# Row maxima of two attention heads at a time, from matmuls on the two halves of TensorE's rows

## The chip, the cores and the metric

The kernel runs on one core of a Trainium2 chip. The metric is the device time of one execution in microseconds (us). Times are shown as the median of several runs; one further execution was taken with the profiler on, and all rows below come from it.

## The reference

One layer of a hybrid decoder, 2048 tokens of width 1024 behind 16 learned meta tokens (L = 2064 rows), in float32:

```python
h = layer_norm(concat(meta, x))
q, k, v, f_logit, g_att, u, g_pool = split(h @ w_in)
# forgetting attention, 16 heads of 64
c = cumsum(log_sigmoid(f_logit + b_f))              # per head, along the rows
s = q @ k.T / 8 + c[:, None] - c[None, :]           # causal
a = softmax(s) @ v * silu(g_att)
# pooling mixer: trailing means over 2, 4, 8, 16 rows, a small linear map, a scale
p = multiscale_pool(u) * silu(g_pool)
out = layer_norm(alpha * h + concat(a, p) @ w_out)[16:]
```

What the change touches is the softmax. For its exponentials the kernel wants, for each row of q, the largest logit beforehand. The term c of the query's own row is the same for all keys of the row and drops out; the term of the key, −c, does not, and has to be in the maximum.

## The kernel before

Matrix products are made to float32 precision out of pairs: each operand is split into a high part (hh, wh, ka, qa; float32r, which TensorE reads) and a low part (hl, wl, lo), and `mm3` issues three matmuls for one product (high by high, low by high, high by low).

The program has three stages. First the input is normalised and transposed, and v is projected (to about 290 us). Then comes the stretch of the projections (about 328 to 1290 us), which the change touches. Then the attention itself, which reads q, k and the maxima back from a DRAM tensor kqd, with the output projection filled in between (from about 1320 us).

In the second stretch a list of jobs is worked off in order. Each job projects 128 columns of w_in over all rows, in chunks (`proj`): 8 steps k, each one `mm3`, into one of two PSUM tiles d. Jobs are: `qk_job`, 16 times, one a head (64 columns of k beside 64 of q, five chunks of 412 or 416 rows); `gp_job` and `u_job`, 8 times each (gate and input of the pooling mixer); `ga_job`, 8 times (gate of the attention). gp_job and ga_job have four chunks of 512 rows, u_job five of 412 or 416. Weights of the next job are fetched and split in the middle of the job before.

After each chunk `qk_job` evicts k and q: ScalarE writes the high parts into ka and qa, VectorE the low parts into lo, and three transfers bring them to kqd. ka and qa have 64 rows of the head and two more: rows 64 and 65 of ka hold the key's forget term in two parts (loaded from kqd), those of qa are ones. So one matmul of 66 rows gives the logits with the forget term in them.

The maxima are found in pieces (`max_piece`): a row block i of 128 queries against the keys of a range p of up to 1024 positions. Range 0 starts at position 112, so block i has 128i + 144 keys over its ranges. A piece is one or two matmuls (512 columns at most each) into a PSUM tile mx of 1024 columns, of which there are two; VectorE adds a causal mask to the last 128 columns of a block's last range (mask_q), and one TENSOR_REDUCE over the piece writes a column of mxs. `max_end` joins the ranges, transposes the 16 columns and sends them to kqd rows 258 and 259.

Pieces are spread between the projection's steps: a queue `pend`, and `tick()` behind every step, which collects a credit and takes an entry off the queue for each whole credit. The credit of a step is 0.3, or, outside of a head's own job ("tail"), the length of the queue over the steps that are left until the next head's first chunk, if that is more. What is left then is emptied at once. [...]

## Time and profile before

| what | value |
|---|---|
| time, median of 3 runs | 2349.0 us (2347.35 to 2353.8) |
| the profiled execution: time, span | 2348.34 us, 2346.6 us |
| TensorE matmul busy | 2266.2 us, 97% of the span |
| VectorE, ScalarE, GpSimd busy | 1464.9, 978.3, 783.6 us |
| granted TensorE clock, mean | 0.99 |
| matmuls into mx (maxima) | 704 |
| reductions mxs<-mx on VectorE | 416, 359.5 us |

Busy time of an engine is the time in which at least one of its instructions is under way. Matmuls overlap in the array, so the listed length of one (its way through the pipeline) is longer than the time by which it holds up the next; that time is the distance between two starts. PEld are the loads of the stationary operand, which each matmul has. The helper that records every instruction gives them all one line, L86, so groups are told apart by their tiles.

### The profile page before, as it was taken

Reading aid. Unit: us, or ns where it says so; the run is one execution under the profiler, and the core shown is the slowest. Engines: PE = TensorE matmul, PEld = TensorE weight load, DVE = VectorE, ACT = ScalarE, POOL = GpSimd, SP = SyncE. Lnnn points to the kernel's source line nnn. Section 1 sums busy time; section 2 is a strip of 40 time slices with the busy share of each in tenths; the row PEclk is TensorE's granted clock in tenths of the full one; section 3 lists DMA queues with packets and bytes.
Section 4 is the critical chain, followed back from the end, with each engine's and each line's share of the span. In section 5 each row is a group of like instructions: output and inputs, shape, how many; then the busy total and the mean of one; then the engine's idle time right before and its main releaser. Section 6 shows DMA issues by size and latency. Waiting matters only on the chain.

```text
span 2346.6 us, 32233 instructions
## 1 busy us (share of the span) xinstructions
PE 2266.2 (97%) x11146; PEld 1902.4 (81%) x11146; DVE 1464.9 (62%) x2360; ACT 978.3 (42%) x1895; POOL 783.6 (33%) x624
## 2 busy tenths in 40 slices
PE   6999999999999999999999799999999999999998
PEld 4878799999999999999888577777777777776787
DVE  5521246755766567656634388787878777767347
ACT  4421421222212212211111387878878877776000
POOL 4700021222313404140010146555565655545000
PEclk9999999999999999999999899999999999999999
DMA  6743532222222222222222766675767767555955
GB/s 228 226 140 105 154 97 63 91 65 85 89 63 91 82 72 85 62 96 81 80 69 70 194 188 195 192 212 171 201 193 200 207 194 222 167 163 178 290 186 168
DMA packets 347778, 335.41 MB, mean 143 GB/s; under 512 B 57888, under 2 KB 271344, under 8 KB 347584
## 3 DMA queue, kind: packets, MB, share of 16 engines
q1 hardware_dynamic: 347616, 333.37, 47.0%
q8 instruction: 88, 1.44, 0.3%
q14 instruction: 74, 0.61, 0.1%
HBM read 209.15 MB, written 124.13 MB: 142 GB/s over the span
## 4 chain that ended last, share of the span: by engine, by line
PE 90%; DVE 3%; DMA 2%; issue 2%; ACT 2%; POOL 1%; SPq 0%; DVEq 0%; ACTq 0%; POOLq 0%
PE d L86 61%; PE s L86 11%; PE yo L86 7%; PE mx L86 6%; PE xo L86 5%; DVE pl L86 1%; PE fz L86 1%; PE tr L86 1%; DMA xm<-xa 1%; ACT ph L86 1%; DMA wst<-in_wout_dram 0%; SPq L86 0%; POOL acc L86 0%; ACT s L86 0%; POOL araw L86 0%
## 5 line engine op out<-in xcount | busy, mean ns | idle before, releaser
L86 PE MATMUL d<-hh,wh 128*128 128x412 f32 (+2 forms) x1472 | 543.6, 369 | 0.0
L86 PE MATMUL d<-hl,wh 128*128 128x412 f32 (+2 forms) x1472 | 538.3, 366 | 0.0
L86 PE MATMUL d<-hh,wl 128*128 128x412 f32 (+2 forms) x1472 | 537.9, 365 | 0.0
L86 DVE TENSOR_TENSOR pl<-s,ph 128x512 fp32r<-128x512 f32 (+3 forms) x592 | 373.5, 649 | 166.8 <-ACT s L86 158.2
L86 DVE TENSOR_REDUCE mxs<-mx 128x1 f32<-128x912 f32 (+14 forms) x416 | 359.5, 865 | 85.9 <-PE mx L86 76.1
L86 ACT ACTIVATE ph<-s 128x512 fp32r<-128x512 f32 (+3 forms) x592 | 336.9, 569 | 156.4 <-PE s L86 141.9
L86 PE MATMUL d<-wh,xm 128*128 128x512 f32 x1024 | 348.1, 397 | 4.2 <-DMA xm<-xa 3.4
L86 ACT ACTIVATE s<-s 128x512 f32<-128x512 f32 (+3 forms) x592 | 335.7, 567 | 0.0
L86 PEld LDWEIGHTS d<-hl,wh 128*128 128x128 f32 x1472 | 277.7, 189 | 24.8
L86 PEld LDWEIGHTS d<-hh,wh 128*128 128x128 f32 x1472 | 276.9, 188 | 23.0 <-ACT gst L86 0.3
L86 PEld LDWEIGHTS d<-hh,wl 128*128 128x128 f32 x1472 | 276.6, 188 | 23.3
L86 POOL TENSOR_TENSOR wl<-wst,wh 128x1024 fp32r<-128x1024 f32 x40 | 96.2, 2405 | 589.7 <-ACT wh L86 564.1
L86 PE MATMUL s<-qa,ka 68*128 68x512 f32 (+3 forms) x640 | 244.8, 383 | 21.5 <-DVE pl L86 21.1
L86 PE MATMUL yo<-pl,vt 128*66 128x512 f32 (+3 forms) x640 | 229.1, 374 | 11.3 <-ACT c L86 11.0
L86 PE MATMUL s<-qb,kb 128*128 128x512 f32 (+3 forms) x640 | 234.6, 367 | 0.0
L86 PE MATMUL xo<-ph,vt 128*128 128x512 f32 (+3 forms) x640 | 232.6, 367 | 0.0
L86 PEld LDWEIGHTS d<-wh,xm 128*128 128x128 f32 x1024 | 193.7, 190 | 47.1 <-issue 4.2
L86 POOL TENSOR_TENSOR tu<-ph 128x512 f32<-128x512 f32 x144 | 188.3, 1308 | 99.5 <-ACT ph L86 95.4
L86 PE MATMUL d<-wl,xm 128*128 128x512 f32 x512 | 203.1, 397 | 0.0
L86 PE MATMUL mx<-ka,qa 66*128 66x512 f32 (+5 forms) x704 | 198.2, 348 | 3.4 <-ACT qa L86 3.4
L86 PEld LDWEIGHTS s<-qa,ka 68*128 68x128 f32 x640 | 122.4, 191 | 61.4 <-DVE pl L86 33.7
L86 DVE TENSOR_TENSOR mx<-mx,mask_q 128x128 f32<-128x128 f32 x256 | 76.5, 299 | 117.8 <-PE mx L86 115.1
(185 smaller groups left out, 3097.4 us busy)
## 6 DMA issues: line engine op xcount, KB each, us to landing
xm<-xp SPq DMA_DIRECT2D x32, 1024.0 KB
xm<-xa SPq DMA_DIRECT2D x20, 1024.0 KB
vd<-vs SPq DMA_DIRECT2D x32, 512.0 KB
vt<-vd SPq DMA_DIRECT2D x64, 256.0 KB
qb<-kqd SPq DMA_DIRECT2D x64, 256.0 KB
xa<-am SPq DMA_DIRECT2D x32, 512.0 KB
xp<-pm SPq DMA_DIRECT2D x32, 412.0 KB
kqd<-lo SPq DMA_DIRECT2D x64, 206.0 KB
```

Source lines behind the costliest of these rows:

```text
L86: return in_order(f(*a, **k))
```

## The change

`k_job` and `q_job` take the place of `qk_job`, 8 times each, one pair of heads g: the first projects 128 columns of k (two heads), the second 128 of q. Head 2g lies on rows 0 to 63 of the tiles kp and qr, head 2g+1 on rows 64 to 127. A chunk is evicted by one ScalarE and one VectorE instruction, and four transfers bring it to kqd.

A piece now serves both heads. Their matmuls, of 64 rows each, are issued in turn, the first head's into one mx tile and the second's into the other; there are still two such tiles. The rows of the forget term are gone. Instead the term is kept in DRAM as fk, a row for each head, and `fb_load` brings the range that is due, broadcast to 128 partitions, into fb0 and fb1 (one buffer each). For each head VectorE adds the mask as before and then runs one tensor_tensor_reduce: logits plus fb, written back to the mx tile, with the maximum read out into mxs.

The pieces of range 0 are queued while q is projected, at 0.2 credits a step; then come the load of range 1, two empty entries, the nine pieces of range 1, the load of range 2, an empty entry, its one piece, and the end: of these 26 pieces a pair six fall into the q job. The queue is empty during k_job. The jobs between the pairs are three (gp, u, ga) for groups 0 to 5, two (gp, u) for group 6 and four for group 7, of which the last is done when the pools of the attention are open. The first job is now k_job 0 in place of gp_job 0; the forget chain runs inside it. The buffer pm of the pool job is one where it was two.

```diff
     kqd = dtile("kqd", [H, 260, L], F32)
+    fk = dtile("fk", [H, L], F32)
...
+        dma(fk.rearrange("h (s t) -> (h s) t", s=8), zf)
...
-        sched["credit"] += max(0.3, len(pend) / max(sched["steps"], 1) if sched["tail"] else 0.0)
+        sched["credit"] += max(sched["rate"], len(pend) / max(sched["steps"], 1) if sched["tail"] else 0.0)
...
+                fbs[e] = fbp.tile([P, 1024], F32, tag=f"fb{e}", name="fb")
+                dma(
+                    fbs[e][:, lo - 1024 * p : hi - 1024 * p],
+                    fk[2 * g + e : 2 * g + e + 1, lo - 112 : hi - 112].broadcast_to([P, hi - lo]),
+                )
...
-            ps = psm.tile([P, 1024], F32, tag="mx", name="mx", bufs=2)
+            pss = [psm.tile([P, 1024], F32, tag="mx", name="mx", bufs=2) for e in range(2)]
             v = lo
             while v < hi:
-                e = min(hi, 512 * (v // 512 + 1))
-                diag = e == P * i + 256
-                mm(
-                    ps[:, v - base : e - base], qa[:, NM + P * i : NM + P * (i + 1)],
-                    ka[:, v - 112 : e - 112], start=True, stop=True,
-                )
-                if diag:
-                    d = ps[:, e - P - base : e - base]
-                    nc.vector.tensor_tensor(out=d, in0=d, in1=mask_q, op=ALU.add)
-                v = e
-            nc.vector.tensor_reduce(
-                out=mx[:, p, i : i + 1], in_=ps[:, lo - base : hi - base], axis=AX.X, op=ALU.max
-            )
+                end = min(hi, 512 * (v // 512 + 1))
+                for e in range(2):
+                    r = slice(DH * e, DH * (e + 1))
+                    mm(
+                        pss[e][:, v - base : end - base], qr[r, NM + P * i : NM + P * (i + 1)],
+                        kp[r, v - 112 : end - 112], start=True, stop=True,
+                    )
+                v = end
+            sl = slice(lo - base, hi - base)
+            for e in range(2):
+                ps = pss[e]
+                if hi == P * i + 256:
+                    d = ps[:, hi - P - base : hi - base]
+                    nc.vector.tensor_tensor(out=d, in0=d, in1=mask_q, op=ALU.add)
+                nc.vector.tensor_tensor_reduce(
+                    out=ps[:, sl], in0=ps[:, sl], in1=fbs[e][:, sl], scale=1.0, scalar=-3.0e38,
+                    op0=ALU.add, op1=ALU.max, accum_out=mx[:, p, e, i : i + 1],
+                )
...
-            nc.scalar.copy(out=kd_, in_=ps[0:DH, :])
-            nc.scalar.activation(out=qd_, in_=ps[DH:P, :], func=AF.Copy, scale=0.125)
+            nc.scalar.copy(out=kp[:, c0:c1], in_=ps)
...
-                pm = qp.tile([P, 2, 416], F32R, tag="pm", name="pm", bufs=2)
+                pm = qp.tile([P, 2, 416], F32R, tag="pm", name="pm")
...
+    for g in range(H // 2):
+        jobs += [(k_job, g, wqk[2 * g]), (q_job, g, wqk[2 * g + 1])]
+        n = 3 if g < 6 else 2 if g == 6 else 4
```

On TensorE, in a projection with pieces between its steps, before. Here d<-... are the projection's matmuls and mx<-ka,qa the pieces; the size is that of the matmul's result:

```order
L86 MATMUL mx<-ka,qa 128x400
L86 MATMUL mx<-ka,qa 128x512
L86 MATMUL d<-hh,wh 128x412
L86 MATMUL d<-hl,wh 128x412
L86 MATMUL d<-hh,wl 128x412
L86 MATMUL d<-hh,wh 128x412
L86 MATMUL d<-hl,wh 128x412
L86 MATMUL d<-hh,wl 128x412
L86 MATMUL mx<-ka,qa 128x512
L86 MATMUL mx<-ka,qa 128x384
```

And in the changed program, from the gp job into the u job of a group (x2 is one matmul for each of the two heads):

```order
L86 MATMUL mx<-kp,qr 128x400 x2
L86 MATMUL mx<-kp,qr 128x512 x2
L86 MATMUL d<-hh,wh 128x512
L86 MATMUL d<-hl,wh 128x512
L86 MATMUL d<-hh,wl 128x512
L86 MATMUL d<-hh,wh 128x512
L86 MATMUL d<-hl,wh 128x512
L86 MATMUL d<-hh,wl 128x512
L86 MATMUL d<-hh,wh 128x512
L86 MATMUL d<-hl,wh 128x512
L86 MATMUL d<-hh,wl 128x512
L86 MATMUL d<-hh,wh 128x416
```

Pieces come half as often and have twice the matmuls, those of the two heads next to each other.

On VectorE before, across a chunk of a head's job (lo are the low parts, mask_q the causal mask):

```order
L86 TENSOR_TENSOR lo<-d,ka 64x412
L86 SCALAR_TENSOR_TENSOR lo<-d,qa 64x412
L86 TENSOR_REDUCE mxs<-mx 128x1
L86 TENSOR_TENSOR mx<-mx,mask_q 128x128
L86 TENSOR_REDUCE mxs<-mx 128x1 x2
```

And in the changed program, at a u job (s<-... are its own two instructions a chunk; ISA mx,mxs<-mx,fb is the tensor_tensor_reduce, ISA mxs the reading out of its maximum):

```order
L86 ISA mx,mxs<-mx,fb 128x912
L86 ISA mxs 128x1
L86 ISA mx,mxs<-mx,fb 128x912
L86 ISA mxs 128x1
L86 SCALAR_TENSOR_TENSOR s<-s,u 128x412
L86 SCALAR_TENSOR_TENSOR s<-s,psc_t,sg 128x412
L86 ISA mx,mxs<-mx,fb 128x912
L86 ISA mxs 128x1
```

One reduction became two instructions, and those of the two heads stand in a row.

On SP's queue in the changed program, at the end of a q job and after it (kqd the chunks, wst weights, xp the pool job's result, gd the attention's gate, fb the broadcast forget terms):

```order
L86 DMA kqd<-qr 64x412 x2
L86 DMA kqd<-lo 64x412 x2
L86 DMA wst<-in_wga_dram 128x1024
L86 DMA fb<-fk 128x1024 x2
L86 DMA wst<-in_wqk_dram 128x1024
L86 DMA xp<-pm 128x2x400
L86 DMA xp<-pm 128x2x412 x3
```

The broadcasts, which before were not there, stand ahead of weights and of the pool job's results, and wait for the last reduction that reads the buffer.

## The prediction, made before the changed kernel was run

> **What bounds the kernel now.** I read the page first (busy shares, then the chain that ended last), then busy time by stretch, then the timeline of TensorE inside the stretch that the change touches.

> ```profile
> span 2346.6 us, 32233 instructions
> PE 2266.2 (97%) x11146; PEld 1902.4 (81%) x11146; DVE 1464.9 (62%) x2360; ACT 978.3 (42%) x1895; POOL 783.6 (33%) x624
> PE 90%; DVE 3%; DMA 2%; issue 2%; ACT 2%; POOL 1%; SPq 0%; DVEq 0%; ACTq 0%; POOLq 0%
> PE d L86 61%; PE s L86 11%; PE yo L86 7%; PE mx L86 6%; PE xo L86 5%; DVE pl L86 1%; PE fz L86 1%; PE tr L86 1%; DMA xm<-xa 1%; ACT ph L86 1%; DMA wst<-in_wout_dram 0%; SPq L86 0%; POOL acc L86 0%; ACT s L86 0%; POOL araw L86 0%
> ```

> TensorE carries the span. The next rows are the stretch of the projections, where the row maxima are found: first all work, then the maxima (tile mx) alone; then what TensorE waited for there.

> ```profile
> 328.00:1290.00 962.00, 958.61 (x4775) 881.31 (x4774) 584.80 (x949) 187.72 (x363) 215.36 (x167) 1.00 0.25 79
> 328.00:1290.00 962.00, 198.16 (x704) 132.75 (x704) 434.50 (x672) 1.00 0.25 79
> PE mx L86 <- ACT qa L86: 3.4, 4, 1.1
> ```

> The columns after the length are PE, PEld, DVE, ACT and POOL (in the second row PE, PEld, DVE), then clock, DMA share, GB/s. TensorE idles 3.4 us of 962, at the full clock, so a microsecond of TensorE saved or added here is one of the end. VectorE has 377 us free. Busy time of PE counts overlapping pipelines; what a matmul really takes is the distance of two starts:

> ```profile
> 1018.57 0.39 PE L86 MATMUL d<-hh,wl 128*128 128x512 f32 x1
> 1018.80 0.58 PE L86 MATMUL mx<-ka,qa 66*128 66x400 f32 x2
> 1019.22 0.40 PE L86 MATMUL d<-hh,wh 128*128 128x512 f32 x1
> 1019.45 0.40 PE L86 MATMUL d<-hl,wh 128*128 128x512 f32 x1
> 1021.09 0.39 PE L86 MATMUL d<-hh,wl 128*128 128x512 f32 x1
> 1021.32 0.63 PE L86 MATMUL mx<-ka,qa 66*128 66x512 f32 x2
> 1021.98 1.22 DVE L86 TENSOR_REDUCE mxs<-mx 128x1 f32<-128x1024 f32 x1 [1.18 <-PE mx L86]
> 1023.87 0.23 PE L86 MATMUL mx<-ka,qa 66*128 66x128 f32 x1
> 1023.93 0.44 PE L86 MATMUL d<-hh,wh 128*128 128x512 f32 x1
> ```

> From 1019.22 to 1021.32 nine matmuls of 512 columns start: 0.233 us each, 0.455 ns a column. A piece of 400 and 512 columns holds TensorE from 1018.80 to 1019.22, 0.42 us, the same price. Weight loads hide, except behind a very short matmul (1023.87, 0.06 us long; the next one is lengthened to 0.44).

> **The change part by part.**

> Columns. A row block i of a head needs 128i+144 columns, 17,664 a head, 282,624 in all, in 416 pieces: 128.6 us. Afterwards the two heads of a pair stand on rows 0 to 63 and 64 to 127 and their matmuls are issued in turn, in 208 pieces. If the two run at once, a pair streams its columns in the time of one head: −64 us. Nothing before puts two matmuls side by side, so the bounds are 0 and −64; I take −64, because the operands share no row and write different PSUM tiles.

> Going in and out of half rows. One place before uses fewer than half of the rows: the last 16 rows of the input are transposed by eight matmuls between full ones.

> ```profile
> 129.45 0.39 PE L86 MATMUL d<-wvl,hh 128*128 128x512 f32 x1
> 129.45 0.19 PEld L86 LDWEIGHTS d<-wvh,hl 128*128 128x128 f32 x1
> 129.68 0.40 PE L86 MATMUL d<-wvh,hl 128*128 128x512 f32 x1
> 130.01 0.56 PEld L86 LDWEIGHTS tr<-ident,xt 16*128 16x128 f32 x8 [0.36 <-issue]
> 130.01 0.66 PE L86 MATMUL tr<-ident,xt 16*128 16x16 f32 x8
> 130.60 0.19 PEld L86 LDWEIGHTS d<-wvh,hh 128*128 128x128 f32 x1
> 130.60 0.50 PE L86 MATMUL d<-wvh,hh 128*128 128x512 f32 x1
> 130.71 0.19 PEld L86 LDWEIGHTS d<-wvl,hh 128*128 128x128 f32 x1
> 130.94 0.40 PE L86 MATMUL d<-wvl,hh 128*128 128x512 f32 x1
> ...
> L86 PEld LDWEIGHTS tr<-ident,xt 16*128 16x128 f32 x8 | 0.6, 136 | 0.4 <-issue 0.4
> ```

> Among full matmuls a load starts with the matmul ahead of it (129.45). Here no load starts at 129.68; that matmul streams until 129.91 and the first 16-row load comes at 130.01: 0.10 us empty, for no data ("issue"). The eight loads span 0.56 us, each 0.136 long, so one follows the other by 0.06. Coming back, the last of the eight starts at about 130.46 (0.66 less its 0.21); the full load comes at 130.60, some 0.09 after that transpose's own 0.05, and the matmul beside it lasts until the next start at 130.94: 0.34 in place of 0.23, so 0.11 for a load that nothing hides. Transposes that use all rows but few columns show none of this:

> ```profile
> 558.77 0.39 PE L86 MATMUL d<-hh,wl 128*128 128x512 f32 x1
> 559.00 0.27 PE L86 MATMUL tr<-ident,mxs 128*16 128x128 f32 x1
> 559.03 0.43 PE L86 MATMUL d<-hh,wh 128*128 128x416 f32 x1
> 559.30 0.35 PE L86 MATMUL d<-hl,wh 128*128 128x416 f32 x1
> ```

> So I price one pair piece at 0.10 (empty) + 0.06 (first head's load) + 0.06 (second head's load, by which its stream starts later) + 0.09 + 0.11 (way out) = 0.42 us; 208 × 0.42 = +87 us. Bounds: 0 if half rows need no such break (every all-row shape above), and 0.52 us = 108 us if a half-row load takes the 0.11 of a full one. I take 0.42, since 64 rows are like the 16 in using part of the array. [...]

> Short pieces. Five of a head's segments have 144 columns or fewer and expose some 0.045 us of the next load (0.44 at 1023.93 against 0.40): 80 × 0.045 = −3.6 us, as that load is in the 0.11 now. ACT evicts a chunk in one instruction, not two: −3 us of the 3.4 us wait.

> VectorE. The forget term leaves the matmul (66 rows to 64) and is added in the reduction, which reads PSUM and a broadcast row, writes PSUM back, and reads its maximum out in a second instruction.

> ```profile
> L86 DVE TENSOR_REDUCE mxs<-mx 128x1 f32<-128x912 f32 x160 | 177.1, 1107 | 66.4 <-PE mx L86 64.9
> L86 DVE TENSOR_REDUCE mxs<-mx 128x1 f32<-128x1024 f32 x32 | 39.2, 1224 | 11.8 <-PE mx L86 11.2
> L86 DVE TENSOR_REDUCE mxs<-mx 128x1 f32<-128x512 f32 x16 | 11.1, 691 | 0.6
> L86 DVE TENSOR_TENSOR pl<-s,ph 128x512 fp32r<-128x512 f32 x448 | 302.8, 686 | 125.7 <-ACT s L86 122.0 <-PE s L86 0.3
> L86 DVE TENSOR_TENSOR mx<-mx,mask_q 128x128 f32<-128x128 f32 x256 | 76.5, 299 | 117.8 <-PE mx L86 115.1
> L86 DVE TENSOR_TENSOR mxs<-mxs 128x9 f32<-128x9 f32 x16 | 2.7, 167 | 0.0
> L86 DVE SCALAR_TENSOR_TENSOR lo<-d,qa 64x412 fp32r<-64x412 f32 x64 | 37.8, 591 | 1.1
> ```

> At 512 columns two inputs (686 ns) cost what a reduction does (691), so the new instruction should keep the old one's time; the read-out lies between 0 and 167 ns (the shortest VectorE row) and I take 100: +42 us. Eighty evictions fewer at 591 ns: −47 us. VectorE stays near 580 of its 962 us.

> But the two PSUM tiles mx no longer alternate between pieces: one pair takes both. The second head of the next piece waits for the second reduction of this one, and all later projection matmuls queue behind it on TensorE. For 912 columns, from free tile to free tile: 0.42 (stream) + 0.20 (two matmuls from 1021.32 stream until 1021.78, their reduction starts at 1021.98) + 2 × 1.21 = 3.05 us. TensorE offers pieces at 0.26 a step in groups 0 to 5 (29 entries over 112 steps): 3.9 steps of three matmuls, 2.7 us at 512 columns, plus 0.84 for the piece: 3.5, no wait; beside the pool job (412 columns, 0.56 a step) 3.0, and that job's own VectorE work comes in the way: an estimated 0.1 to 0.4 on wide pieces, about 2 us a group, 12 in all. Group 6 has 80 steps, 0.36 a step, 2.8 steps: 2.4 to 2.8 us, short by 0.3 to 0.7, and more with the mask's 0.3, on some 13 pieces: 8 us. Group 7, 104 steps: 5 us. Sum +25 us, bounds 0 (pieces narrow enough) and 40 (read-out of 167 ns, pool job's VectorE work in the way).

> DMA. Per pair 934 KB, 1 MB and 131 KB of broadcast rows: 17 MB, at 79 GB/s and a quarter of the engines' time no load. The second broadcast must wait for the last reduction of the first range (2.7 us), then 1 MB at the 197 GB/s that the last stretch moves is 5.3 us:

> ```profile
> 1320.00:2346.00 1026.00, 980.99 (x4784) 751.16 (x4782) 752.45 (x1185) 671.68 (x1343) 472.54 (x384) 0.99 0.66 197
> ```

> Its first reader comes four entries later, 15 steps, 9 us: hidden, by a microsecond only; if that cover goes, VectorE waits, the tiles stay taken, and some 2 us × 8 come on top. On SP's queue the waiting broadcast stands ahead of the gate's stores and the pool's (xp, now with one buffer pm instead of two), behind which ACT would wait; a projection's second PSUM buffer gives 4.5 us of cover. I price both at 0 and keep 20 us for the range. The other job order, the first job and the later end of the forget chain cost nothing that the rows show: projections keep their number and size.

> Sum: −64 − 4 − 3 + 87 + 25 = +41 us on the profiled execution's 2348.3 (its span is 1.7 less), 2389; the median shown, 2349.0, is 0.7 above it: **2390**.

> **Rivals.**
> 1. Half rows need no break, second heads start at once: −64 − 7 + 208 × 0.06 (loads) + 25 = −34, 2315. For it: the break was seen with 16 rows only, in one place. It decides below 0.22 us a pair piece. The faster side.
> 2. The two halves do not run at once: 0 instead of −64, and fewer waits, as pieces are longer (12 for 25): −7 + 87 + 12 = +92, 2441. For it: no matmul before overlaps another.
> 3. The new reduction needs two cycles a column: 2 × (2.06 + 0.1) a wide pair, 282,624 × 1.04 ns = +294 us of VectorE, a free-to-free time of 5.2 us against TensorE's 3.0 to 3.5: about 1.5 to 2 us on most of 208 pieces when narrow ones are left out, some +220, 2600. Against it: the 686 ns of two inputs.
> 4. The breaks are cheap by half (0.22 us) and cancel against the columns: within 0.3%.

> **How the numbers follow.** Forecast as summed (2362 to 2425 by its own bounds) 0.61; rival 1 0.14; rival 2 0.11; rival 3 0.04; rival 4 0.10. About 0.3% (7 us) is what a measurement of this kernel can tell from no change. Faster: rival 1 and a little of 4, 0.17. Same: most of 4 and the forecast's lowest edge, 0.12. Slower: the rest, 0.71. Range 2335 to 2445: it leaves out most of rival 1 and all of 3.

> **What would show it.** In the changed profile: mx matmuls of two heads starting within about 0.1 us and ending together (or one after the other: rival 2); a gap of 0.1 us ahead of each pair and a d matmul of 0.5 us behind it (or neither: rival 1); PE waiting for VectorE at mx, most in group 6; the reduction at about 1.1 us for 912 columns (2.0: rival 3). The prediction is wrong if the break costs under 0.3 us or VectorE becomes the bound.

## The result, and the profile after

The changed kernel takes 2382.4 us (median of 4 runs, 2381.1 to 2384.4); the kernel before took 2349.0 us beside it (2347.35 to 2353.8; a fourth execution of it, of 5709 us, stands apart and is not counted). The ratio is 1.014, 95% interval 1.0124 to 1.0156. The profiled execution took 2384.4 us, its span is 2382.7, 36.1 us more than before's.

The page of the changed kernel: span, busy shares, and the chain that ended last by engine and by tile.

```profile
span 2382.7 us, 32409 instructions
PE 2296.2 (96%) x11138; PEld 1830.6 (77%) x11138; DVE 1403.7 (59%) x2671; ACT 934.5 (39%) x1806; POOL 780.0 (33%) x624
PE 83%; DVE 4%; issue 4%; DMA 3%; ACT 2%; POOL 2%; SPq 1%; ACTq 0%; DVEq 0%; POOLq 0%
PE d L86 57%; PE s L86 10%; PE yo L86 7%; PE mx L86 4%; PE xo L86 4%; DVE mx L86 1%; PE fz L86 1%; ACT ph L86 1%; SPq L86 1%; DVE pl L86 1%; ACT s L86 1%; PE tr L86 1%; POOL s L86 1%; DMA xm<-xa 1%; DMA vt<-vd 0%
```

TensorE still carries the end, but its share of the chain fell from 90% to 83%, and what came in is "issue" (2% to 4%) and VectorE at tile mx. Next, the stretch of the projections: all work, then the maxima alone (PE, PEld, DVE busy, then clock, DMA share, GB/s), and what TensorE waited for at mx (us, times, longest). The maxima now begin at 309.6 us, so 18 of their 704 matmuls lie ahead of this window.

```profile
328.00:1330.00 1002.00, 992.77 (x4791) 813.49 (x4791) 526.32 (x1238) 150.86 (x289) 222.83 (x178) 1.00 0.32 89
328.00:1330.00 1002.00, 131.19 (x686) 61.60 (x686) 420.89 (x652) 1.00 0.32 89
PE mx L86 <- DVE mxs L86: 8.3, 20, 0.9
```

PE looks 99% busy, yet the stretch is longer, so busy time does not tell it: an overlapped or lengthened matmul counts as busy (the d matmul of 742.33 below is listed with 0.50 us, the one behind it with 0.39). The timeline of one piece does (400 and 512 columns a head). First TensorE's matmuls, then the same from a view that ends just behind the second start, then the weight loads.

```profile
741.17 0.40 PE L86 MATMUL d<-hl,wh 128*128 128x512 f32 x1
741.41 0.39 PE L86 MATMUL d<-hh,wl 128*128 128x512 f32 x1
741.73 0.68 PE L86 MATMUL mx<-kp,qr 64*128 64x400 f32 x4
742.33 0.50 PE L86 MATMUL d<-hh,wh 128*128 128x512 f32 x1
742.67 0.39 PE L86 MATMUL d<-hl,wh 128*128 128x512 f32 x1
```

```profile
741.73 0.45 PE L86 MATMUL mx<-kp,qr 64*128 64x400 f32 x2
```

```profile
741.17 0.19 PEld L86 LDWEIGHTS d<-hh,wl 128*128 128x128 f32 x1
741.73 0.30 PEld L86 LDWEIGHTS mx<-kp,qr 64*128 64x128 f32 x4 [0.37 <-issue]
742.33 0.19 PEld L86 LDWEIGHTS d<-hh,wh 128*128 128x128 f32 x1 [0.31 <-issue]
742.44 0.19 PEld L86 LDWEIGHTS d<-hl,wh 128*128 128x128 f32 x1
```

The d matmul of 741.41 streams until 741.64. The loads of both heads come 0.09 us later, at 741.73 (4 ns apart in the records), for no data ("issue"), and both 400-column matmuls start 3 ns apart in the records (the median over all pieces is 4 ns) and end together after 0.45. The two of 512 columns start at 742.016 and 742.019 in the records, 0.29 us behind the first pair where 400 columns stream in 0.18: 0.105 of a load shows. The stream ends at 742.25, the load of the full array comes 0.085 later, and the d matmul beside it holds TensorE for 0.34 in place of 0.23, 0.107 more. The break is thus 0.09 + 0.105 + 0.085 + 0.107 = 0.39 us.

VectorE's groups (count, then busy us and mean ns of one, then the idle time ahead of them), and its idle time ahead of the reductions while the forget term was still on its way (us, times):

```profile
L86 DVE CUSTOM_DVE_ANT_0 mx<-mx,fb 128x912 f32<-128x912 f32 x160 | 174.9, 1131 | 67.9 <-PE mx L86 67.4
L86 DVE CUSTOM_DVE_ANT_0 mx<-mx,fb 128x1024 f32<-128x1024 f32 x32 | 39.0, 1239 | 1.2 <-PE mx L86 0.7
L86 DVE DVE_READ_ACCUMULATOR2_ANT mxs<- 128x1 f32 x416 | 59.0, 142 | 0.0
L86 DVE SCALAR_TENSOR_TENSOR lo<-d,qr 128x412 fp32r<-128x412 f32 x32 | 18.7, 585 | 15.0 <-ACT qr L86 15.0
  DMA fb<-fk: 8.8, 10
```

A ledger of all pieces was made from the records for each kernel. A piece's time is the distance from the start of the last d matmul ahead of it to the start of the second d matmul behind it, less the columns of the two d matmuls at 0.4545 ns (the median distance of two starts in before's records is 0.454 to 0.456 ns a column); "breaks" is the count times the typical 0.398 us (for before: all that is not columns), "waits" what is then left.

| kernel | pieces | their time, us | columns | breaks | waits |
|---|---|---|---|---|---|
| before | 416 | 139.2 | 128.5 | 10.7 | |
| changed | 208 | 169.6 | 64.3 | 82.8 | 22.5 |

Pieces account for +30.4 of the 36.1 us. By the first attention matmul (1316.5 us before, 1350.5 now) the kernel is 34.0 behind, so some 3.6 lie elsewhere in the stretch or ahead of it; 2.1 came in the attention. Of the 3.6, 2.5 stand ahead of the first projection (its first matmul starts at 279.3 us, before's at 276.8; the experiments with 208 and 416 pieces have 276.2 to 278.8), and 1.3 is a single wait between two projection matmuls at 1199 us.

### The profile page after: what moved, and what is told of

The parts are those of the page before. It is cut to its first block, busy times and chain, and to the rows that moved or that the text cites. A ratio compares the mean times of both kernels' runs of the same rounds, so it can differ in the third digit from the quotient of the medians.

```text
span 2382.7 us, 32409 instructions
## 1 busy us (share of the span) xinstructions
PE 2296.2 (96%) x11138; PEld 1830.6 (77%) x11138; DVE 1403.7 (59%) x2671; ACT 934.5 (39%) x1806; POOL 780.0 (33%) x624
## 4 chain that ended last, share of the span: by engine, by line
PE 83%; DVE 4%; issue 4%; DMA 3%; ACT 2%; POOL 2%; SPq 1%; ACTq 0%; DVEq 0%; POOLq 0%
PE d L86 57%; PE s L86 10%; PE yo L86 7%; PE mx L86 4%; PE xo L86 4%; DVE mx L86 1%; PE fz L86 1%; ACT ph L86 1%; SPq L86 1%; DVE pl L86 1%; ACT s L86 1%; PE tr L86 1%; POOL s L86 1%; DMA xm<-xa 1%; DMA vt<-vd 0%
## 5 line engine op out<-in xcount | busy, mean ns | idle before, releaser
L86 PE MATMUL d<-hh,wh 128*128 128x412 f32 (+2 forms) x1472 | 560.3, 381 | 1.6 <-DVE lo L86 1.1
L86 PE MATMUL d<-hl,wh 128*128 128x412 f32 (+2 forms) x1472 | 538.7, 366 | 0.0
L86 PE MATMUL d<-hh,wl 128*128 128x412 f32 (+2 forms) x1472 | 538.0, 366 | 0.0
L86 DVE TENSOR_TENSOR pl<-s,ph 128x512 fp32r<-128x512 f32 (+3 forms) x592 | 373.7, 650 | 167.7 <-ACT s L86 159.1
L86 DVE CUSTOM_DVE_ANT_0 mx<-mx,fb 128x912 f32<-128x912 f32 (+14 forms) x416 | 359.5, 880 | 85.3 <-PE mx L86 68.1
L86 ACT ACTIVATE ph<-s 128x512 fp32r<-128x512 f32 (+3 forms) x592 | 337.4, 570 | 154.5 <-PE s L86 143.1
L86 PE MATMUL d<-wh,xm 128*128 128x512 f32 x1024 | 349.0, 398 | 5.9 <-DMA xm<-xa 5.1
L86 ACT ACTIVATE s<-s 128x512 f32<-128x512 f32 (+3 forms) x592 | 335.5, 567 | 0.0
L86 PEld LDWEIGHTS d<-hh,wh 128*128 128x128 f32 x1472 | 276.2, 188 | 73.5 <-issue 45.3
L86 PEld LDWEIGHTS d<-hh,wl 128*128 128x128 f32 x1472 | 276.7, 188 | 23.3
L86 PEld LDWEIGHTS d<-hl,wh 128*128 128x128 f32 x1472 | 276.8, 188 | 19.4
L86 POOL TENSOR_TENSOR wl<-wst,wh 128x1024 fp32r<-128x1024 f32 x40 | 96.4, 2411 | 526.0 <-ACT wh L86 380.3
L86 PE MATMUL s<-qa,ka 68*128 68x512 f32 (+3 forms) x640 | 245.1, 383 | 19.3 <-DVE pl L86 19.0
L86 PE MATMUL yo<-pl,vt 128*66 128x512 f32 (+3 forms) x640 | 229.4, 374 | 11.7 <-ACT c L86 11.5
L86 PE MATMUL s<-qb,kb 128*128 128x512 f32 (+3 forms) x640 | 234.7, 367 | 0.0
L86 PE MATMUL xo<-ph,vt 128*128 128x512 f32 (+3 forms) x640 | 232.8, 367 | 0.0
L86 PEld LDWEIGHTS d<-wh,xm 128*128 128x128 f32 x1024 | 194.2, 190 | 49.1 <-issue 5.9
L86 POOL TENSOR_TENSOR tu<-ph 128x512 f32<-128x512 f32 x144 | 186.7, 1297 | 97.0 <-ACT ph L86 90.2
L86 PE MATMUL d<-wl,xm 128*128 128x512 f32 x512 | 203.7, 398 | 0.0
L86 DVE TENSOR_TENSOR mx<-mx,mask_q 128x128 f32<-128x128 f32 x256 | 80.7, 315 | 180.7 <-PE mx L86 180.7
L86 PEld LDWEIGHTS s<-qa,ka 68*128 68x128 f32 x640 | 122.4, 191 | 59.5 <-DVE pl L86 32.1
L86 POOL TENSOR_TENSOR acc<-ph 128x512 f32<-128x512 f32 x48 | 65.3, 1361 | 240.2 <-ACT ph L86 240.2
```

Of the source, the lines that this page charges most:

```text
L86: return in_order(f(*a, **k))
```

## Experiments

All were run beside the kernel before, which took 2347.4, 2348.0 and 2350.6 us in the three sittings. First four edits of the changed kernel that take its terms apart: the price of a break, the columns, the pairing, and VectorE.

### One piece for each head

```diff
-    def max_piece(mx, i, p):
+    def max_piece(mx, i, p, e):
...
-            pss = [psm.tile([P, 1024], F32, tag="mx", name="mx", bufs=2) for e in range(2)]
+            ps = psm.tile([P, 1024], F32, tag="mx", name="mx", bufs=2)
...
-                pend.append(max_piece(mx, done, 0))
+                pend.extend(max_piece(mx, done, 0, e) for e in range(2))
...
-    RATE = 0.2
+    RATE = 0.4
```

> The changed kernel with each pair piece cut in two: one piece a head, 64 rows each, put into the queue separately (credit 0.4 a step in place of 0.2, twice the empty entries), with projection matmuls between the two. Theory A (every entry into half rows and every return costs a fixed break, 0.39 us together, whoever runs in it): 416 x 0.39 + 128.5 us of columns = 291 us for the pieces in place of 169.6, and no waits for a free tile; 2382 + 121 = 2503 us. Theory B (the break comes from running two heads beside each other, or from their semaphores): a lone head of 64 rows costs what the 66 rows cost before, 139 us: 2352 us.

Measured: 2502.7 us (2501.2 to 2508.9), ratio 1.0668 [1.0651, 1.0685]. A piece of 144 columns of one head in the timeline:

```profile
751.89 0.35 PE L86 MATMUL d<-hh,wl 128*128 128x412 f32 x1
752.17 0.33 PE L86 MATMUL mx<-kp,qr 64*128 64x144 f32 x1
752.43 0.46 PE L86 MATMUL d<-hh,wh 128*128 128x412 f32 x1
752.73 0.35 PE L86 MATMUL d<-hl,wh 128*128 128x412 f32 x1
```

From 751.89 to 752.73 are 0.84 us, of which 2 × 0.187 are the two d matmuls of 412 columns and 0.065 the 144 columns: 0.40 for the break. All 416 pieces take 291.9 us, 128.5 of them columns: 0.393 a piece. So the price is one of the excursion and not of the pairing: one head alone pays as much as two. The second head's load and start add nothing that shows (0.398 us for the two together). Theory A gave 2503 us and is met; theory B, 2352, fell.

### All rows in the matmuls

```diff
-                        pss[e][:, v - base : end - base], qr[r, NM + P * i : NM + P * (i + 1)],
-                        kp[r, v - 112 : end - 112], start=True, stop=True,
+                        pss[e][:, v - base : end - base], qr[:, NM + P * i : NM + P * (i + 1)],
+                        kp[:, v - 112 : end - 112], start=True, stop=True,
```

> The changed kernel with all 128 rows in each maximum's matmul (both heads' rows at once, so the maxima are those of the sum of the two heads' logits; everything else is as in the changed kernel). Theory A: no break, columns one after the other: 128.5 + 8 us of pieces and about 12 us of waits for a free tile in place of 169.6: 2361 us, the price of the rest of the change about +10 us on the kernel before. Theory C (what the change lost lies in the rest of it: job order, broadcasts, the fused reduction, one pm buffer): the columns no longer overlap, +64 us: 2446 us.

Measured: 2372.3 us (2370.4 to 2376.5), ratio 1.0112 [1.0096, 1.0129]. The piece of 400 and 512 columns, and the waits:

```profile
738.76 0.39 PE L86 MATMUL d<-hh,wl 128*128 128x512 f32 x1
739.00 0.98 PE L86 MATMUL mx<-kp,qr 128*128 128x400 f32 x4
739.82 0.39 PE L86 MATMUL d<-hh,wh 128*128 128x512 f32 x1
740.05 0.40 PE L86 MATMUL d<-hl,wh 128*128 128x512 f32 x1
...
PE mx L86 <- DVE mxs L86: 12.5, 22, 1.0
```

The break is gone on both sides: the piece starts 0.24 us behind the d matmul ahead of it, and the first d matmul behind it holds TensorE for its plain 0.23. Twice the columns without a break (both heads' logits are then summed in each tile) are about 10 us *faster* than half the columns with one (11.0 us by the ledger; the intervals of the two ratios just touch). The kernel before fits this: its matmuls of 66 rows, in pieces of 400 and 512 columns, take 0.005 us over their columns (median of 160). Theory C, 2446 us, fell. Theory A stands, but it missed by 11 us: the waits did not shrink. A piece is now 0.82 us of columns where it was 0.42 of columns and 0.40 of break, so the next one comes no later for VectorE. The pieces take 158.6 us, some 24 of it waits.

### Head by head inside a piece

```diff
-            v = lo
-            while v < hi:
-                end = min(hi, 512 * (v // 512 + 1))
-                for e in range(2):
-                    r = slice(DH * e, DH * (e + 1))
+            for e in range(2):
+                r = slice(DH * e, DH * (e + 1))
+                v = lo
+                while v < hi:
+                    end = min(hi, 512 * (v // 512 + 1))
```

> The changed kernel with the matmuls of a pair piece issued head by head (all segments of the first, then all of the second) in place of in turn. Theory A (matmuls start in the order in which they stand, and one half must be done with a segment before its next starts): the second head starts only when the first head's second segment does, so each piece of two segments is longer by its first one: 104 x 0.182 + 40 x 0.233 = +28 us, less a few that the waits take up: 2405 us. Theory D (the two halves run through their own queues): no difference, 2382 us.

Measured: 2379.2 us (2377.6 to 2387.9), ratio 1.0144 [1.0123, 1.0165], the changed kernel's time within the intervals. The program order of a piece is now 400, 512 (first head), 400, 512 (second). The timeline, and the same in a view that ends behind the second start:

```profile
741.28 0.40 PE L86 MATMUL d<-hh,wl 128*128 128x512 f32 x1
741.61 0.69 PE L86 MATMUL mx<-kp,qr 64*128 64x400 f32 x4
742.23 0.50 PE L86 MATMUL d<-hh,wh 128*128 128x512 f32 x1
```

```profile
741.61 0.45 PE L86 MATMUL mx<-kp,qr 64*128 64x400 f32 x2
```

The two that start at 741.61 are both of 400 columns: the second head's first matmul runs 7 ns behind the first head's, and ahead of the first head's 512 columns (741.900 in the records), which stand before it in the program. Theory A, which had the streams in program order and 2405 us, fell; D's 2382 us is met. In 112 of the 128 pieces whose two segments differ in width, the first segments of both heads start before either second one. Between the two orders of issue the time shows no difference.

### A short reduction

```diff
+                sr = slice(max(lo, hi - P) - base, hi - base)
                 nc.vector.tensor_tensor_reduce(
-                    out=ps[:, sl], in0=ps[:, sl], in1=fbs[e][:, sl], scale=1.0, scalar=-3.0e38,
+                    out=ps[:, sr], in0=ps[:, sr], in1=fbs[e][:, sr], scale=1.0, scalar=-3.0e38,
```

> The changed kernel with the reduction over the last 128 columns of each piece alone (the maxima leave the other keys out; matmuls, masks, loads and the number of instructions stay). Theory A (22 us of the pieces' time is TensorE waiting for a tile that VectorE has not given back): these waits go, 2382 - 22 = 2360 us. Theory E (VectorE is never late enough to matter): 2382 us.

Measured: 2357.7 us (2354.9 to 2364.4), ratio 1.0049 [1.003, 1.0068]. VectorE's groups, and what is left of the waits:

```profile
L86 DVE CUSTOM_DVE_ANT_0 mx<-mx,fb 128x128 f32<-128x128 f32 x416 | 120.6, 306 | 202.2 <-PE mx L86 188.6 <-DMA fb<-fk 4.9
PE mx L86 <- DVE mxs L86: 0.6, 1, 0.6
```

With VectorE out of the way the pieces take 148.1 us: 64.3 + 208 × 0.397 + 1.2. So 21 of the 22.5 us of waits were VectorE's, as theory A had it, and what is left is the change's own balance: 148.1 against 139.2 before, still a loss. At 0.4545 ns a column a break of 0.398 us is worth 876 columns; a piece here saves 679 on average (17,664 × 8 / 208). So I tried to save breaks.

### Fewer, fuller pieces

```diff
+    SPANS = ((0, 1008), (1008, 2016), (2016, L))
...
+    def packed(p):
+        lo, hi = SPANS[p]
+        pieces = [[]]
+        pos = 0
+        for i in range(NM):
+            k, end = lo, min(hi, P * i + 144)
+            while k < end:
+                if pos == 1024:
+                    pieces.append([])
+                    pos = 0
+                n = min(end - k, 512 - pos % 512)
+                pieces[-1].append((i, pos, k, k + n))
+                k += n
+                pos += n
+        return pieces
...
+                for i in sorted({t[0] for t in segs}):
...
+                    nc.vector.tensor_tensor_reduce(
...
-    RATE = 0.2
+    RATE = 0.15
+    WU = 0.7
```

> The columns of neighbouring blocks are packed into full pieces of 1024 columns a head (19 pieces a pair of heads in place of 26: 152 in all for 208), with the forget term loaded for 1008 keys at a time; the pieces are issued every 6.7 ticks (9.5 beside the wider filter jobs) in place of 5. Theory A (what the change costs is a price per break of 0.398 us, paid at the entry to and the exit from a piece, whatever its length): the pieces take 152 x 0.398 = 60.5 us beside 64.3 us of columns, and some 4 us for the loads of short segments at block borders inside a piece; with the waits for the mx tiles (22.5 us) gone through the wider spacing that is 129 us where the changed kernel's took 169.6, so 2382 - 41 = 2341 us, from 2336 to 2350. Theory B (VectorE is the limit: a piece has 2.2 blocks a head, so 672 reductions in place of 416, each with about 0.16 us fixed and 0.142 us of read-out, 78 us more): the waits stay at 22 us or grow, 2364 us or above. Theory C (a new block inside a piece changes the stationary rows, and that drains as a break does, some 0.2 us each x 23 a pair x 8 = 37 us): 2378 us.

> The packed kernel, but each row-maximum reduction takes only the last 128 columns of its block's part of a piece (the rest of the maximum is left out), so that VectorE is never late. Theory A: the same as the packed kernel within 4 us, since its waits are already gone, 2337 to 2345 us. Theory B: 15 to 25 us below the packed kernel. Theory C: 2374 us, as a drain on TensorE does not care for VectorE.

Measured: 2469.5 us (2466.5 to 2474.6), ratio 1.0523 [1.0505, 1.0541], and with the short reduction 2392.0 (2388.3 to 2400.0), ratio 1.0195 [1.0174, 1.0216]. Theory B's "or above" leaves room for the first, and no theory had the size of either. The edit also drops empty entries at a pair's end and joins more columns of partial maxima there; these were not priced apart. What happens at the second range shows in VectorE's timeline of the packed kernel, the first piece of five blocks (its first four and last two rows out of 28, both heads one after the other) and then TensorE's:

```profile
524.75 0.20 DVE L86 TENSOR_TENSOR mx<-mx,mask_q 128x32 f32<-128x32 f32 x1 [6.18 <-PE mx L86]
524.99 0.20 DVE L86 CUSTOM_DVE_ANT_0 mx<-mx,fb 128x32 f32<-128x32 f32 x1
525.11 0.14 DVE L86 DVE_READ_ACCUMULATOR2_ANT mxs<- 128x1 f32 x1
525.28 0.30 DVE L86 TENSOR_TENSOR mx<-mx,mask_q 128x128 f32<-128x128 f32 x1
...
531.41 0.30 DVE L86 CUSTOM_DVE_ANT_0 mx<-mx,fb 128x128 f32<-128x128 f32 x1
531.62 0.14 DVE L86 DVE_READ_ACCUMULATOR2_ANT mxs<- 128x1 f32 x1
```

```profile
528.46 0.42 PE L86 MATMUL mx<-kp,qr 64*128 64x416 f32 x1
531.91 1.32 PE L86 MATMUL mx<-kp,qr 64*128 64x416 f32 x5 [3.02 <-DVE mxs L86]
533.16 0.79 PE L86 MATMUL d<-hh,wh 128*128 128x512 f32 x1
533.76 0.63 PE L86 MATMUL d<-hl,wh 128*128 128x512 f32 x1
...
PE mx L86 <- DVE mxs L86: 57.5, 42, 3.0
```

Each block's part asks a mask, a reduction and a read-out of VectorE, 0.5 us even for 32 columns (524.75 to 525.28), so that this piece holds it for 7.0 us. The next piece's second head waits for its tile, TensorE idles for 3.02 us, and then the d matmuls are long: 0.63 in place of 0.40, with 0.43 from one start to the next in place of 0.23. The granted clock by windows of the same place (the third number from the right, ahead of DMA share and GB/s; the first number behind the length is PE's busy time):

```profile
526.00:528.50 2.50, 2.47 (x14) 2.01 (x12) 2.29 (x11) 0.00 (x0) 0.00 (x0) 1.00 0.01 3
528.50:532.00 3.50, 0.47 (x3) 0.23 (x3) 3.26 (x14) 0.00 (x0) 0.00 (x0) 0.92 0.00 0
532.00:536.00 4.00, 4.00 (x12) 2.98 (x13) 3.75 (x11) 1.04 (x3) 1.93 (x2) 0.50 0.11 42
536.00:540.00 4.00, 4.00 (x19) 2.93 (x17) 1.09 (x3) 0.00 (x0) 0.00 (x0) 0.72 0.17 64
540.00:543.00 3.00, 3.00 (x13) 2.19 (x13) 2.79 (x12) 0.00 (x0) 0.00 (x0) 1.00 0.00 0
```

TensorE was busy for 0.47 us of the 3.50 to 532.00, and the clock is at 0.50 from there to 536.00; with the shares of the windows on both sides (0.92 and 0.72, read as parts at 1.00 and at 0.50) that is an estimated 6.8 us at half. The ledger: 229.9 us of pieces, 60.3 more than the changed kernel's, and outside of the pieces 145 d matmuls at about half speed (over 1.7 times their plain time) with 25.2 us lost: together about the 85.1 us by which the spans differ. Theory B named the cause, VectorE, and was far too low. The short reduction leaves the masks and read-outs, and so the waits in part: pieces 172.1 us, 8.1 lost to the clock. Theory C is excluded by the pieces that did not wait: those of two blocks cost mostly 0.46 to 0.50 us over their columns, 0.06 to 0.10 above a plain break and not 0.2, and those of five blocks 0.62, which is 0.06 for each of their four block borders.

### Merged pieces

Here no block is split, so VectorE keeps its number of instructions.

```diff
-    def max_piece(mx, i, p):
+    def max_piece(mx, blocks, p):
...
-        pend.extend(max_piece(mx, i, 1) for i in range(7, NM))
+        pend.extend(max_piece(mx, b, 1) for b in SECOND)
...
-    RATE = 0.2
+    RATE = 0.16
+    FIRST = [(0, 1), (2, 3)] + [(i,) for i in range(4, NM)]
+    SECOND = [(13, 7), (12, 8), (11, 9), (10,), (14,), (15,)]
```

> No block is split: pairs of short blocks share a piece (0 with 1, 2 with 3, and in the second range of keys 13 with 7, 12 with 8, 11 with 9), 21 pieces a pair of heads in place of 26, 168 in all for 208; issue rate 0.16 a tick for 0.2. The reductions take only the last 128 columns of a block's part (the rest of the maximum is left out), as in the kernel with the short reduction, so that VectorE is out of the way. Theory A (0.398 us a break, and nothing else): 40 breaks fewer than the kernel with the short reduction, 2357.7 - 15.9 = 2342 us, 2338 to 2346. Theory B (what was saved comes back as waits at the pieces that follow one with two blocks a head, whose masks and reductions take VectorE about twice as long): 5 such pieces a pair, 40 in all, at 0.5 us or more each: 2362 us or above.

> The same with the whole reduction, which computes what the changed kernel computes. Theory A: 40 breaks fewer and the waits as in the changed kernel (22.5 us): 2382.4 - 15.9 = 2366.5 us, 2360 to 2372. Theory B: a piece with two blocks a head holds VectorE for 4.2 us (2 heads x (1024 columns x 1.053 ns + 2 x 0.16 fixed + 2 x 0.2 for read-outs and 0.315 for a mask)), longer than the distance to the next piece at some places, so the waits grow by 1 us at 40 places: 2406 us.

Measured with the short reduction: 2359.0 us (2356.0 to 2359.6), ratio 1.0036 [1.0024, 1.0049], not told apart from 208 pieces with it. The ledger says why: 143.3 us of pieces = 64.3 + 168 × 0.400 + 11.7 us of waits. Forty breaks did go, at the price of theory A, and most of it came back as waits at the pieces behind those of two blocks (theory B in kind; it had put them at 0.5 us or more at each of 40, 2362 or above; the late ones are 16). With the whole reduction: 2413.2 us (2408.6 to 2414.7), ratio 1.0265 [1.0251, 1.0279]; theory B, 2406, is near: it had 40 us more of waits where the ledger has 34.5, and nothing for the clock. Of the 57 us of waits in all, 50 stand behind pieces of two blocks. The waits, and PE's busy time and the clock around two of them:

```profile
PE mx L86 <- DVE mxs L86: 33.6, 36, 1.6
380.00:382.50 2.50, 1.22 (x6) 0.62 (x4) 2.38 (x9) 0.00 (x0) 0.00 (x0) 1.00 0.00 0
382.50:386.00 3.50, 3.21 (x17) 2.70 (x18) 3.36 (x11) 1.04 (x3) 1.56 (x2) 1.00 0.01 2
386.00:388.50 2.50, 0.85 (x2) 0.35 (x2) 2.36 (x8) 0.00 (x0) 0.37 (x1) 1.00 0.44 169
388.50:391.00 2.50, 2.50 (x9) 2.30 (x9) 2.43 (x7) 0.00 (x0) 0.00 (x0) 0.55 0.03 7
391.00:394.00 3.00, 3.00 (x13) 2.04 (x11) 0.07 (x1) 1.04 (x3) 1.94 (x2) 0.81 0.08 30
```

Here 61 d matmuls at half speed lose another 9.8 us. None of these versions beats the kernel before. Without any wait, 168 pieces would need 64.3 + 67 = 131 us against its 139, a gain of 8 us at most. With the whole maximum the waits came with them in the one order that was run, which puts three pieces of two blocks one behind the other; whether they stay when these alternate with single blocks was not tried.

| kernel | time, us | pieces | their time | waits | lost to the clock |
|---|---|---|---|---|---|
| changed | 2382.4 | 208 | 169.6 | 22.5 | 0 |
| one piece a head | 2502.7 | 416 | 291.9 | with the breaks | 0 |
| all rows | 2372.3 | 208 | 158.6 | about 24 | 0 |
| head by head | 2379.2 | 208 | 168.0 | 21 | 0 |
| short reduction | 2357.7 | 208 | 148.1 | 1.2 | 0 |
| packed | 2469.5 | 152 | 229.9 | 105 | 25.2 |
| packed, short | 2392.0 | 152 | 172.1 | 47 | 8.1 |
| merged, short | 2359.0 | 168 | 143.3 | 11.7 | 0 |
| merged | 2413.2 | 168 | 188.0 | 57 | 9.8 |

Waits are here what columns and breaks of 0.398 us leave of the pieces' time. In the two packed rows this holds some 10 us of loads at block borders besides.

## Why the prediction was right, point by point

It said 2390 by +41 on the profiled execution; that rose by 36.1 (2348.3 to 2384.4). The direction and the two large terms hold, and some of the small ones are wrong in size. That the total is near is in part luck: against the forecast the break came out 4.2 us lower, the waits 2.5 lower and the short pieces with ACT up to 3.7 lower, while 5.7 us came in places that were not priced.

- **Columns, −64.** Measured −64.2 (128.5 to 64.3 us): the two heads stream side by side, their starts 4 ns apart in the median. Rival 2 fell with the first timeline above. Its estimate of the waits, 12 in place of 25, was not tested: no run has a piece of both heads with the columns one after the other and the break besides.
- **Break, 208 × 0.42 = +87.** Measured 208 × 0.398 = 82.8. The total came right by two errors that nearly cancel. The way in was to be 0.10 empty, 0.06 for the first head's load and 0.06 for the second's; it is 0.09 and 0.105, and nothing for the second, since the loads of both heads start 4 ns apart. The row of 16-row loads was the wrong neighbour for the load; the full array's 0.11, given there as the upper bound, was the right one. The way out, 0.09 + 0.11, is 0.085 + 0.107. Rivals 1 and 4 fell: they needed 0.22 us or less. All rows against half rows show where it comes from: no break with the one, 0.398 us with the other.
- **Waits, +25.** Measured 22.5, and 21 of them are shown by the short reduction, which takes them away. Their places were met too: groups 0 to 5 were put at 12 us, group 6 at 8 and group 7 at 5, and the ledger has 9.2, 8.2 and 5.2. In groups 0 to 5 more than half is one piece a group beside the pool job (0.83 us, where 0.1 to 0.4 had been estimated): that job's own two instructions on VectorE, 1.23 us, stand ahead of the reductions that free the tile.
- **Short pieces and ACT, −7.** All that before's pieces cost beyond their columns is 10.7 us: about 4 at the short segments, 4.4 at four waits for ACT, the rest spread thin. In the changed kernel a short piece costs the plain break (0.386 to 0.408 us), so all 10.7 went.
- **VectorE.** The reduction takes 1131 ns where before's took 1107, as said; the read-out takes 142 ns, not 100. VectorE was to stay near 580 us busy in the stretch; over the whole span the lengths of its instructions add up to 6 us more than before, but its busy time fell by 61 (1403.7 for 1464.9): read-outs overlap their neighbours (at 525.11 in the packed kernel one starts before the reduction of 524.99 ends), so lengths added up overstate what they cost. Rival 3, with twice the 1.04 ns a column that before's rows give (691 ns at 512 columns, 1224 at 1024), fell: the new instruction's rows give 1.05 (700 and 1239 ns).
- **DMA and SP at 0.** The broadcasts were not quite hidden: VectorE waited 8.8 us for fb in ten places. Whether any of it reached TensorE was not told apart; in the kernel with the short reduction it waited 4.9 us and TensorE almost none. The 3.6 us beyond the pieces, placed above, and the 2.1 us in the attention were not priced, and their causes were not sought.

## What to carry to other kernels

Putting two heads on the two halves of the rows halved the time of the columns here (128.5 to 64.3 us), but each excursion from full-array matmuls and back cost 0.398 us, 876 columns of this kernel: count the columns that an excursion saves (here 679 on average, 1024 in a full piece), and do it in few long ones or not at all; no version here gained by it. Ask of fewer and fuller pieces whether the engine that frees their PSUM tiles keeps pace; here VectorE did not, and most of what the breaks saved, or more, came back as waits: of the 15.9 us of forty breaks 4.8 were left with the short reduction (148.1 to 143.3 us of pieces), and with the whole one the pieces took 18.4 more (169.6 to 188.0). Costs of a new mode are best taken from the row that is like it in each part, the load apart from the empty time ahead of it, since a total can come right through errors that cancel.
